# The first modulation vectors computed in two halves of the features, and the token streams loaded ahead of the other transfers

## The chip, the cores and the metric

The kernel runs on one core of a Trainium2 chip. The metric is the device time of one execution in microseconds; a kernel's time is the median of its runs. TensorE (PE in the profile) multiplies matrices, with its weight loads listed apart as PEld; VectorE (DVE) and ScalarE (ACT) work on tiles; GpSimd (POOL) and SyncE (SP) are used here mostly to issue transfers. PEq, ACTq and SPq are the sequencers that issue for these engines. Each engine runs its instructions in the order in which the program was laid out.

## The reference, cut to what matters

The model has two layers and two token streams of 1024 features each: 512 latent tokens (x) and 256 context tokens (ctx). Each layer derives six modulation vectors of 1024 features for each stream from a conditioning vector, and the first thing that a layer does is to normalise each token, scale and shift it by two of these vectors, and multiply the result by one wide input matrix:

```
ml = (silu(c) @ w_ada[l] + b_ada[l]).reshape(B, 6, 1, 1024)      # latent stream
mc = (silu(c_ctx) @ w_ada[l] + b_ada[l]).reshape(1, 6, 1, 1024)  # context stream
hl = rmsnorm(xl, norm1[l]) * (1 + ml[:, 1]) + ml[:, 0]
hc = rmsnorm(xc, norm1[l]) * (1 + mc[:, 1]) + mc[:, 0]
pl, pc = split_in(hl @ w_in[l]), split_in(hc @ w_in[l])
```

Mixing of three kinds, an output product, a gated residual and a feed-forward part follow. w_ada[l] is 1024 x 6144 float32. Vectors 0 and 1 (shift and scale) are wanted at the head of the layer, 2 to 5 much later.

## The kernel before

Tokens lie along the free dimension, features over 128 partitions, so a stream is eight feature tiles (k = 0 to 7) of 128 x 512 (latent) or 128 x 256 (context). Every float32 operand of a large product is cut into a rounded part and a rest (hi and lo), and a product takes three matmuls, hi by hi, lo by hi and hi by lo.

**The modulation vectors** come from `ada(l, g, ring)` (L580). Group g holds two vectors: group 0 is shift and scale of the first norm. Its part of w_ada is 8 MB and comes as 16 tiles of 512 KB: for each half f of the 2048 columns, and each k, one transfer on the queue of SyncE (L588) and matmuls on narrow column strips of TensorE (L590) that sum over k into one bank of PSUM, bank 2 ("a"). In the layout before, half f = 0 is the whole shift vector and f = 1 the whole scale vector. After all 16 tiles one copy brings the bank to SBUF (L594), four transposes turn it (L597), four small additions add the bias (L605), and two operations form gain times (1 + scale) (L611).

**The head of layer 0** is `project` (L691). It loads both streams on the queue of ScalarE (`x_load`, L497: four transfers for each), computes the norm of each stream (`rstd`, L618: squares on ScalarE, sums on VectorE, then `token_rstd` L633 with two steps on TensorE, L637 and L645, which leaves the factors of all tokens in a PSUM bank), runs `ada(0, 0)` to its end with a ring of eight buffers, and then `modulated` (L648) for the context and after it the latent stream: for each k two operations on VectorE (L655, L659) with one on ScalarE between them (L658).

**The token-wise product** is `product_n` (L560), called by `project_dn`: a product with 400 columns in which the tokens of a cell of 128 are the rows. There are six cells, two of context and four of latent tokens, each with an open sum in a bank of its own (0, 1, 3, 4, 5, 6). The weights come in four pieces (k0 = 0, 2, 4, 6), each of two feature tiles; for each piece all six cells get six matmuls (L572, L573, L574), so 144 in all. A piece is loaded (L538), rounded by ScalarE (L540) and its rest formed by VectorE (L541); there are two buffers for each of these steps. When k0 = 6 is done a cell is copied out (`evac`, L727 to L731), with one transfer by GpSimd from one of two small buffers (`ev`). After it come feature-wise products (`product_t`, L544) with convolutions. Beside all this run the 16 tiles of `ada(0, 1)`, with a ring of two buffers.

**Order.** Python generators fix the order of the program; each yields a cost, and `run` (L274) goes on with the one that is furthest behind. On top of that the framework lays out each engine's instructions by a timeline that it simulates: among what is ready it takes the smallest priority number, which grows along the program. `high_priority(n)` and `ahead` (L523) lower the number by n; weight pieces have 500. The order within an engine is fixed then, and on the chip an engine waits at an instruction whose inputs are late, even where later ones are ready. Buffers are found by `Mem` (L173), which prefers those that were freed longest ago.

## Time and profile of the kernel before

| what | us |
|---|---|
| median of 3 runs | 2103.03 (2101.80 to 2104.22) |
| profiled execution | 2102.51 |
| its span, first to last instruction | 2100.70 |
| TensorE busy in the span | 1975.3 (94%) |
| VectorE, ScalarE, GpSimd busy | 1220.2, 858.2, 148.8 |
| mean granted TensorE clock | 0.964 of full speed |

The page gives busy time by engine, then by 40 slices of the span, then DMA, then the chain of work that ended last and the costliest groups of instructions. Ends of matmuls are modelled, so neighbouring matmuls overlap in the listing; the distance between two starts is the better measure of what one takes. Stages are best read from the view by windows, which gives busy time, granted clock and DMA traffic of any stretch, and from the timeline.

### The profile page before, as it was taken

The page shows a single profiled execution, that of the slowest core. Times are in us where ns is not written, and L with a number is a line of the kernel's source. Part 1 is how long each engine was busy: PE and PEld are TensorE (multiplying, and loading weights), DVE is VectorE, ACT ScalarE, POOL GpSimd, SP SyncE. Part 2 cuts the span into 40 slices and gives each one's busy share as a digit, 9 for nine tenths or more (in the row PEclk, how much of TensorE's full clock was granted, in tenths as well). Part 3 has the DMA queues.
Part 4 walks back from the last instruction along what each step waited for, and adds up shares of the span by engine and source line. Part 5 has one row for each costly group of instructions (what it writes and reads, how often), then busy time and mean ns, then how long its engine had stood idle before and what let it go on. Part 6 is the DMA issues. An engine that isn't in the chain of part 4 may idle for free.

```text
span 2100.7 us, 38043 instructions
## 1 busy us (share of the span) xinstructions
PE 1975.3 (94%) x15506; PEld 1626.0 (77%) x15506; DVE 1220.2 (58%) x2761; ACT 858.2 (41%) x1705; POOL 148.8 (7%) x289
## 2 busy tenths in 40 slices
PE   5899999999899999799999998999889979999996
PEld 2787889879899997688788876767678747888885
DVE  4574883756976676766333334756787473333335
ACT  2432354335556563452524232425554234233241
POOL 0001333000000000011000000011200000000000
PEclk9999997999999999899999998999999989999998
DMA  8435343164333242343222245363300222222222
GB/s 338 157 111 166 91 129 105 45 231 152 101 103 110 100 159 86 112 134 118 81 100 90 100 152 173 120 211 131 111 2 12 72 70 91 100 91 100 93 88 81
DMA packets 72831, 242.46 MB, mean 115 GB/s; under 512 B 10320, under 2 KB 13520, under 8 KB 72528
## 3 DMA queue, kind: packets, MB, share of 16 engines
q1 hardware_dynamic: 57456, 196.31, 27.8%
q0 software_dynamic: 12176, 35.19, 5.3%
q10 hardware_dynamic: 3024, 8.53, 1.2%
q8 instruction: 122, 2.00, 0.4%
q14 instruction: 53, 0.43, 0.1%
HBM read 218.21 MB, written 19.14 MB: 113 GB/s over the span
## 4 chain that ended last, share of the span: by engine, by line
PE 79%; DVE 8%; DMA 6%; issue 5%; ACT 2%; POOL 1%; POOLq 0%; ACTq 0%; DVEq 0%; SPq 0%
PE psum L554 20%; PE psum L556 19%; PE psum L555 19%; PE psum L590 2%; PE psum L1457 2%; PE psum L1448 1%; DMA arena<-in_ada 1%; PE psum L1395 1%; PE psum L1122 1%; DVE weights L541 1%; DMA arena<-in_wout 1%; PE psum L1084 1%; DVE arena L1278 1%; DMA r<-in_ada 1%; PE psum L1080 1%
## 5 line engine op out<-in xcount | busy, mean ns | idle before, releaser
L554 PE MATMUL psum<-r,weights 128*128 128x512 f32 (+1 forms) x2288 | 823.2, 361 | 10.8 <-ACT arena L730 3.4
L556 PE MATMUL psum<-r,weights 128*128 128x512 f32 (+1 forms) x2288 | 819.4, 359 | 2.7 <-DVE weights L541 2.5
L555 PE MATMUL psum<-r,weights 128*128 128x512 f32 (+1 forms) x2288 | 817.9, 358 | 0.4 <-DVE r L659 0.3
L540 ACT CAST weights<-arena 128x1024 fp32r<-128x1024 f32 (+3 forms) x295 | 293.7, 996 | 689.1 <-PE psum L555 592.0
L541 DVE TENSOR_TENSOR weights<-arena,weights 128x1024 fp32r<-128x1024 f32 (+3 forms) x295 | 340.8, 1156 | 297.5 <-ACT weights L540 288.8
L554 PEld LDWEIGHTS psum<-r,weights 128*128 128x128 f32 x2288 | 432.3, 189 | 94.7 <-issue 11.1
L556 PEld LDWEIGHTS psum<-r,weights 128*128 128x128 f32 x2288 | 432.1, 189 | 74.1 <-DVE weights L541 6.8
L555 PEld LDWEIGHTS psum<-r,weights 128*128 128x128 f32 x2288 | 432.2, 189 | 68.0 <-issue 3.0
L1514 DVE SCALAR_TENSOR_TENSOR arena<-psum,arena 128x512 f32<-128x512 f32 (+1 forms) x94 | 61.9, 659 | 190.8 <-PE psum L556 190.6
L1501 DVE TENSOR_TENSOR r<-arena,r 128x512 fp32r<-128x512 f32 (+1 forms) x96 | 57.4, 601 | 38.0 <-ACT r L1500 37.7
L658 ACT ACTIVATE r<-arena 128x512 fp32r<-128x512 f32 (+1 forms) x56 | 33.1, 628 | 73.4 <-DVE arena L655 73.4
L590 PE MATMUL psum<-arena 128*32 128x256 f32 x576 | 51.9, 410 | 10.5 <-DMA arena<-in_ada 9.8
L1499 ACT ACTIVATE arena<-arena 128x512 f32<-128x512 f32 (+1 forms) x96 | 54.0, 564 | 2.4
L1500 ACT CAST r<-arena 128x512 fp32r<-128x512 f32 (+1 forms) x96 | 52.8, 553 | 2.4
L1395 PE MATMUL psum<-r 128*128 128x256 f32 (+1 forms) x256 | 52.0, 318 | 0.6 <-ACT r L1428 0.6
L1498 ACT ACTIVATE arena<-psum 128x512 f32<-128x512 f32 (+1 forms) x96 | 50.2, 523 | 0.0
L1485 DVE SCALAR_TENSOR_TENSOR arena<-psum,arena 128x512 f32<-128x512 f32 (+1 forms) x40 | 27.7, 696 | 35.2 <-PE psum L556 34.9
L572 PE MATMUL psum<-weights,r 128*128 128x400 f32 x96 | 34.8, 376 | 10.7 <-DVE arena L655 10.1
L590 PE MATMUL psum<-r,arena 128*32 128x256 f32 x192 | 23.7, 511 | 19.1 <-DMA r<-in_ada 18.9
L655 DVE SCALAR_TENSOR_TENSOR arena<-arena,psum 128x512 f32<-128x512 f32 (+1 forms) x56 | 33.0, 628 | 13.8 <-PE psum L645 13.7
L1453 ACT COPY arena<-psum 128x512 f32<-128x512 f32 x53 | 31.1, 589 | 22.4 <-PE psum L1448 21.9
L1457 PE MATMUL psum<-arena 128*64 128x128 f32 x456 | 37.7, 288 | 2.2 <-ACT arena L1441 2.2
(436 smaller groups left out, 2634.5 us busy)
## 6 DMA issues: line engine op xcount, KB each, us to landing
arena<-in_ff SPq DMA_DIRECT2D x192, 512.0 KB, 3.2
arena<-in_ada SPq DMA_DIRECT2D x72, 512.0 KB, 4.8
arena<-in_win SPq DMA_DIRECT2D x51, 512.0 KB, 3.9
r<-in_ada SPq DMA_DIRECT2D x24, 512.0 KB, 5.5
arena<-in_wout SPq DMA_DIRECT2D x16, 512.0 KB, 3.6
arena<-in_win SPq DMA_DIRECT2D x12, 400.0 KB, 3.6
arena<-in_x ACTq DMA_DIRECT2D x8, 512.0 KB, 7.0
arena<-arena POOLq DMA_DIRECT2D x40, 64.0 KB, 4.5
```

Of the source, the lines that this page charges most:

```text
L540: nc.scalar.copy(hi, st)
L541: nc.vector.tensor_tensor(out=lo, in0=st, in1=hi.bitcast(F32), op=ALU.subtract)
L554: nc.tensor.matmul(o, lhsT=hi[:, w], rhs=h.hi(k), start=k == 0, stop=False)
L555: nc.tensor.matmul(o, lhsT=hi[:, w], rhs=h.lo(k), start=False, stop=False)
L556: nc.tensor.matmul(o, lhsT=lo[:, w], rhs=h.hi(k), start=False, stop=k == nk - 1)
L590: nc.tensor.matmul(ps[32 * j:32 * j + 32, f * 256:f * 256 + 256], lhsT=self.csil[:, k, :], rhs=st[:, j * 256:j * 256 + 256], start=k == 0, ...
L1395: nc.tensor.matmul(o, lhsT=qs[:, kv], rhs=ks[:, kv, a, c0:c1], start=a == 0, stop=a == 1 and not more)
L1457: nc.tensor.matmul(py[heads[kv]], lhsT=self.vS[:, blocks[k0 + kt], heads[kv]], rhs=PT[:, c:c + 128], start=k0 + kt == 0, stop=k0 + kt == n ...
L1499: nc.scalar.activation(out=t, in_=t, func=AF.Square)
L1500: nc.scalar.copy(f.hi(k), t)
L1501: nc.vector.tensor_tensor(out=f.lo(k), in0=t, in1=f.hi(k).bitcast(F32), op=ALU.subtract)
L1514: nc.vector.scalar_tensor_tensor(out=seg.x[m], in0=ps, scalar=self.mod(l, 5, m, seg), in1=seg.x[m], op0=ALU.mult, op1=ALU.add)
```

## The change

The columns of w_ada are laid out anew, for every layer and group: half f of a group's tiles now holds the half f (512 features) of both vectors of the group, instead of the whole of one vector. `ada` is cut into `ada_sums` (the tiles and matmuls of one half) and `ada_out` (two transposes, four bias additions of four columns each, and the products with the gain for that half). Groups other than the first still copy the bank once, and then call `ada_out` twice.

Layer 0 begins with a new function, `project_first`, in place of `project`. The streams are loaded on SyncE's queue with a priority of 2000 instead of on ScalarE's; the tokens' factors are copied from PSUM to SBUF by ScalarE; the first half's eight tiles are summed, its vectors formed (transposes into bank 7, "y"), and the feature tiles k = 0 to 3 of both streams modulated. Then the second half's tiles are summed, with the pieces k0 = 0 and k0 = 2 of the token-wise product set into the program after the second and the sixth of them. After that the second half's vectors and k = 4 to 7 follow, and the rest of the token-wise product is handed to `project_dn`, which runs beside `ada(0, 1)` as before. The streams' buffers are freed only when all tiles are modulated.

```diff
--- before.py
+++ after.py
@@ -155,7 +155,7 @@
     for k, s in PARAM_SHAPES.items():
         assert prm[k].shape == (128,) + s, (k, prm[k].shape)
     o["prm"] = np.concatenate([prm[k].reshape(128, -1) for k in PARAM_SHAPES], axis=1)
-    o["ada"] = w_ada.reshape(DEPTH, 8, 128, 3, 2048).transpose(0, 3, 1, 2, 4)
+    o["ada"] = w_ada.reshape(DEPTH, 8, 128, 3, 2, 2, 512).transpose(0, 3, 1, 2, 5, 4, 6).reshape(DEPTH, 3, 8, 128, 2048)
     o["win"] = np.stack([np.concatenate([_piece(w_in[l][:, IN_COLS[n]]).reshape(-1) for n in IN_NAMES]) for l in range(DEPTH)])
     o["wout"] = np.stack([np.stack([_piece(w_out[l][Y_ROWS][:, 128 * m:128 * m + 128]) for m in range(8)]) for l in range(DEPTH)])
     o["ff1"] = np.stack([np.stack([_piece(w_ff1[l][:, 128 * m:128 * m + 128]) for m in range(32)]) for l in range(DEPTH)])
@@ -489,12 +489,12 @@
         self.wl = Ring(self.wmem, 2, 1024)
 
 
-    def x_load(self, seg):
+    def x_load(self, seg, queue=None):
         seg.xb = [self.get(2 * seg.T, True) for _ in range(4)]
         seg.x = []
         for i, b in enumerate(seg.xb):
             t = b.v.rearrange("p (a t) -> p a t", a=2)
-            self.nc.scalar.dma_start(out=t, in_=seg.home[:, 2 * i:2 * i + 2, :])
+            (queue or self.nc.scalar).dma_start(out=t, in_=seg.home[:, 2 * i:2 * i + 2, :])
             seg.x += [t[:, 0], t[:, 1]]
 
     def x_store(self, seg):
@@ -581,35 +581,44 @@
 
         nc = self.nc
         ps = self.bank("a")
-
         for f in range(2):
-            for k in range(8):
-                st = ring()
-                nc.sync.dma_start(out=st, in_=self.io["ada"][l, g, k, :, f * 1024:f * 1024 + 1024])
-                for j in range(4):
-                    nc.tensor.matmul(ps[32 * j:32 * j + 32, f * 256:f * 256 + 256], lhsT=self.csil[:, k, :], rhs=st[:, j * 256:j * 256 + 256],
-                                     start=k == 0, stop=k == 7, tile_position=(0, 32 * j))
-                yield 2.0
+            yield from self.ada_sums(l, g, f, ring, ps)
         sb = self.get(512)
         nc.vector.tensor_copy(sb.v, ps)
         pt = self.bank("a")
-        for q in range(4):
-            nc.tensor.transpose(pt[:, q * 128:q * 128 + 128], sb.v[:, q * 128:q * 128 + 128], self.ident)
+        for f in range(2):
+            self.ada_out(l, g, f, sb.v, pt[:, f * 256:f * 256 + 256])
         sb.free()
-        m = self.mods[l][:, g * 16:g * 16 + 16, :]
-        src = pt.rearrange("p (f q j r) -> p f j q r", f=2, q=2, j=4)[:, :, :, :, 0:2]
-        b = self.p["b_ada"][:, l, g * 16:g * 16 + 16]
-        for s in range(2):
-            for f in range(2):
-                c = slice(8 * f, 8 * f + 8)
-                nc.vector.tensor_tensor(out=m[:, c, s].rearrange("p (j q) -> p j q", j=4), in0=src[:, f, :, :, s],
-                                        in1=b[:, c].rearrange("p (j q) -> p j q", j=4), op=ALU.add)
+
+    def ada_sums(self, l, g, f, ring, ps):
+
+        nc = self.nc
+        for k in range(8):
+            st = ring()
+            nc.sync.dma_start(out=st, in_=self.io["ada"][l, g, k, :, f * 1024:f * 1024 + 1024])
+            for j in range(4):
+                nc.tensor.matmul(ps[32 * j:32 * j + 32, f * 256:f * 256 + 256], lhsT=self.csil[:, k, :], rhs=st[:, j * 256:j * 256 + 256],
+                                 start=k == 0, stop=k == 7, tile_position=(0, 32 * j))
+            yield 2.0
+
+    def ada_out(self, l, g, f, sb, pt):
+        nc = self.nc
+        for q in range(2):
+            nc.tensor.transpose(pt[:, q * 128:q * 128 + 128], sb[:, f * 256 + q * 128:f * 256 + q * 128 + 128], self.ident)
+        src = pt.rearrange("p (q j r) -> p j q r", q=2, j=4)[:, :, :, 0:2]
+        for v in range(2):
+            c = slice(g * 16 + 8 * v + 4 * f, g * 16 + 8 * v + 4 * f + 4)
+            b = self.p["b_ada"][:, l, c].rearrange("p (j q) -> p j q", j=2)
+            for s in range(2):
+                nc.vector.tensor_tensor(out=self.mods[l][:, c, s].rearrange("p (j q) -> p j q", j=2), in0=src[:, 2 * v:2 * v + 2, :, s], in1=b,
+                                        op=ALU.add)
 
         for w, sc, gain in ((0, 1, "n1"), (1, 4, "n2")):
             if sc // 2 == g:
+                t = slice(4 * f, 4 * f + 4)
                 for s in range(2):
-                    nc.vector.scalar_tensor_tensor(out=self.gmul[l][:, w, :, s], in0=self.mods[l][:, sc * 8:sc * 8 + 8, s], scalar=1.0,
-                                                   in1=self.p[gain][:, l, :], op0=ALU.add, op1=ALU.mult)
+                    nc.vector.scalar_tensor_tensor(out=self.gmul[l][:, w, t, s], in0=self.mods[l][:, sc * 8 + 4 * f:sc * 8 + 4 * f + 4, s],
+                                                   scalar=1.0, in1=self.p[gain][:, l, t], op0=ALU.add, op1=ALU.mult)
 
     def mod(self, l, i, k, seg):
         return self.mods[l][:, i * 8 + k, seg.idx:seg.idx + 1]
@@ -650,14 +659,18 @@
         if pb is None:
             pb = self.rstd(seg)
         h = self.split(seg)
-        for k in range(8):
+        self.modulate(l, which, seg, h, pb, range(8))
+        return h
+
+    def modulate(self, l, which, seg, h, pb, ks):
+        nc = self.nc
+        for k in ks:
             t = self.ev(seg.T)
             nc.vector.scalar_tensor_tensor(out=t, in0=seg.x[k], scalar=self.gmul[l][:, which, k, seg.idx:seg.idx + 1], in1=pb,
                                            op0=ALU.mult, op1=ALU.mult)
             sh = self.mod(l, 3 * which, k, seg)
             nc.scalar.activation(out=h.hi(k), in_=t, func=AF.Identity, bias=sh)
             nc.vector.scalar_tensor_tensor(out=h.lo(k), in0=t, scalar=sh, in1=h.hi(k).bitcast(F32), op0=ALU.add, op1=ALU.subtract)
-        return h
 
 
     def in_piece(self, l, name):
@@ -694,16 +707,54 @@
             if seg.x is None:
                 self.x_load(seg)
         pbs = [self.rstd(seg, "n") for seg in segs]
-        if l == 0:
-            ring = Ring(self, 8, 1024)
-            run(self.ada(0, 0, ring))
-            ring.free()
         for seg, pb in zip(segs, pbs):
             seg.h = self.modulated(l, 0, seg, pb)
+            self.projected(l, seg)
+
+    def projected(self, l, seg):
+        self.x_free(seg)
+        seg.r, seg.b, seg.need = {}, {}, seg is self.lat or l < DEPTH - 1
+        if seg is self.ctx:
+            seg.kv0 = l * 256
+
+    def project_first(self, segs):
+
+        nc = self.nc
+        ab = [self.get(seg.nb * 16, True) for seg in segs]
+        for seg in segs:
+            with self.tc.high_priority(2000):
+                self.x_load(seg, nc.sync)
+        factors = []
+        for seg in segs:
+            pb = self.rstd(seg, "n")
+            factors.append(self.get(seg.T, True))
+            nc.scalar.copy(factors[-1].v, pb)
+        ring = Ring(self, 8, 1024)
+        ps, sb = self.bank("a"), self.get(512)
+        run(self.ada_sums(0, 0, 0, ring, ps))
+        sums = self.ada_sums(0, 0, 1, ring, ps)
+        tokens = None
+        for f in range(2):
+            nc.vector.tensor_copy(sb.v[:, f * 256:f * 256 + 256], ps[:, f * 256:f * 256 + 256])
+            self.ada_out(0, 0, f, sb.v, self.bank("y")[:, 0:256])
+            for seg, b in zip(segs, factors):
+                if f == 0:
+                    seg.h = self.split(seg)
+                self.modulate(0, 0, seg, seg.h, b.v, range(4 * f, 4 * f + 4))
+            if f == 0:
+                for seg, b2 in zip(segs, ab):
+                    seg.r, seg.b, seg.need = {}, {"ab": b2}, True
+                self.ctx.kv0 = 0
+                tokens = self.project_tokens(0, segs)
+                for i, _ in enumerate(sums):
+                    if i in (1, 5):
+                        next(tokens)
+        for seg, b in zip(segs, factors):
             self.x_free(seg)
-            seg.r, seg.b, seg.need = {}, {}, seg is self.lat or l < DEPTH - 1
-            if seg is self.ctx:
-                seg.kv0 = l * 256
+            b.free()
+        sb.free()
+        ring.free()
+        return tokens
 
     def reserve(self, segs, *names):
         for seg in segs:
@@ -717,10 +768,11 @@
     def hs(self, segs, needed=False):
         return [(s, s.h) for s in segs if s.need or not needed]
 
-    def project_dn(self, l, segs):
+    def project_tokens(self, l, segs):
         nc = self.nc
         for seg in segs:
-            seg.b["ab"] = self.get(seg.nb * 16, not seg.need)
+            if "ab" not in seg.b:
+                seg.b["ab"] = self.get(seg.nb * 16, not seg.need)
             seg.r["ab"] = seg.b["ab"].v.rearrange("p (b c) -> p b c", b=seg.nb)
 
         def evac(seg, b, ps):
@@ -731,6 +783,9 @@
             nc.gpsimd.dma_start(out=seg.spill[l][3][b * 128:b * 128 + 128, :], in_=t)
 
         yield from self.product_n(l, "abvi", self.hs(segs), evac)
+
+    def project_dn(self, l, segs, tokens=None):
+        yield from tokens or self.project_tokens(l, segs)
         pad, acc = Ring(self, 2, 512 + 4), Ring(self, 2, 512)
         for i, n in ((1, "k"), (2, "v"), (0, "q")):
             for p in range(2):
@@ -1573,9 +1628,9 @@
                 yield from self.delta_prep(l, seg, seg.need)
 
 
-        self.project(0, both)
+        tokens = self.project_first(both)
         self.reserve((lat, ctx), "dk", "dv", "dq")
-        run(self.project_dn(0, both), (ada(0, 1), 0.7))
+        run(self.project_dn(0, both, tokens), (ada(0, 1), 0.7))
         Ub = self.delta_open(both)
         self.reserve((lat, ctx), "sq0", "sq1")
         run(self.ahead(prep(0, both), 3000), (self.project_swa(0, both), 0.6), (ada(0, 2), 0.7))
```

## Rows read from the trace of the kernel before

**Rows 1.** Windows (start:end, us; busy of each engine, instructions; clock; DMA share, GB/s)

```profile
0.00:2.50 2.50, 0.00 (x0) 0.00 (x0) 0.54 (x2) 0.35 (x1) 1.10 (x9) 1.00 0.33 42
2.50:12.50 10.00, 1.08 (x8) 0.23 (x8) 3.07 (x20) 2.63 (x6) 0.00 (x0) 1.00 0.97 359
12.50:40.00 27.50, 16.02 (x92) 6.32 (x96) 14.31 (x50) 8.37 (x17) 0.00 (x0) 0.85 1.03 410
40.00:81.00 41.00, 35.93 (x264) 29.41 (x260) 23.51 (x54) 16.44 (x32) 1.65 (x3) 0.98 0.53 179
```

**Rows 2.** Timeline of TensorE (start, us taken, line, shape, count, [idle before <-releaser])

```profile
31.77 1.87 PE L637 MATMUL psum<-arena 128*128 128x1 f32 x8 [3.89 <-DVE arena L628]
...
41.62 1.99 PE L590 MATMUL psum<-arena 128*32 128x256 f32 x32
...
46.89 0.45 PE L572 MATMUL psum<-weights,r 128*128 128x400 f32 x1 [0.25 <-ACT r L658]
...
74.13 0.34 PE L573 MATMUL psum<-weights,r 128*128 128x400 f32 x1
...
80.33 0.34 PE L574 MATMUL psum<-weights,r 128*128 128x400 f32 x1
```

**Rows 3.** Timeline of all engines, VectorE's work between the sums and the products

```profile
45.13 0.39 DVE L605 TENSOR_TENSOR arena<-psum,arena 128x8 f32<-128x8 f32 x4 [0.75 <-PE psum L597]
45.44 0.29 DVE L611 SCALAR_TENSOR_TENSOR arena<-arena 128x8 f32<-128x8 f32 x2
45.76 0.87 DVE L655 SCALAR_TENSOR_TENSOR arena<-arena,psum 128x256 f32<-128x256 f32 x2
...
53.24 1.40 DVE L655 SCALAR_TENSOR_TENSOR arena<-arena,psum 128x512 f32<-128x512 f32 x2
...
56.10 1.40 DVE L655 SCALAR_TENSOR_TENSOR arena<-arena,psum 128x512 f32<-128x512 f32 x2
```

**Rows 4.** Groups by line on TensorE, 44 to 81 us (busy us, mean ns | idle before)

```profile
L572 PE MATMUL psum<-weights,r 128*128 128x400 f32 x48 | 16.4, 352 | 0.2 <-ACT r L658 0.2
...
L590 PE MATMUL psum<-arena 128*32 128x256 f32 x64 | 4.9, 390 | 4.0 <-DMA arena<-in_ada 3.5 <-DVE arena L605 0.5
```

**Rows 5.** DMA issues of 0 to 44 us (engine, count, KB each, us to landing)

```profile
arena<-in_ada SPq DMA_DIRECT2D x11, 512.0 KB, 9.3
...
arena<-in_x ACTq DMA_DIRECT2D x4, 512.0 KB, 9.4
arena<-in_win SPq DMA_DIRECT2D x4, 400.0 KB, 7.3
arena<-in_ctx ACTq DMA_DIRECT2D x4, 256.0 KB, 9.2
arena<-in_cst POOLq DMA_DIRECT2D x1, 801.0 KB, 9.8
...
arena<-in_prm ACTq DMA_DIRECT2D x1, 136.0 KB, 4.3
```

**Rows 6.** Chain that ended last, in order of time, one tile at full clock

```profile
110.63 0.57 PE psum L590 x8
```

**Rows 7.** Instructions of line 1441 and who waited for it

```profile
  PE psum L1457: 2.2, 2
```

**Rows 8.** Windows of 2.5 us around two idle stretches of TensorE

```profile
27.50:30.00 2.50, 0.38 (x4) 0.00 (x0) 1.89 (x3) 1.82 (x3) 0.00 (x0) 1.00 1.03 411
...
32.50:35.00 2.50, 2.50 (x22) 1.64 (x21) 1.12 (x7) 0.00 (x0) 0.00 (x0) 0.50 1.02 403
...
40.00:42.50 2.50, 2.50 (x36) 1.26 (x32) 0.00 (x0) 0.00 (x0) 0.00 (x0) 0.64 0.25 92
...
85.00:87.50 2.50, 0.21 (x1) 0.00 (x0) 0.00 (x0) 0.00 (x0) 0.00 (x0) 1.00 1.00 397
...
90.00:92.50 2.50, 2.50 (x7) 1.93 (x7) 0.54 (x4) 1.95 (x4) 0.53 (x1) 0.50 0.00 0
```

**Rows 9.** Timeline of TensorE, the wait behind the copies out of the products

```profile
88.26 0.41 PE L918 MATMUL psum<-r,arena 128*64 128x16 f32 x8 [3.04 <-ACT arena L730]
```

## The prediction

> **What bounds the kernel now.** I read the windows first, then the timelines of the head. TensorE is busy 94% of the span, so little is to be had except where it stands still, and the head is the largest such place: of the first 81 us it is busy 53.0 and idle 28.0 [rows 1], of some 125 us idle in all (span less busy time, from the table). The reader should see three stretches. Up to 40 us the transfers are the bound: 359 GB/s from 2.5 to 12.5 us, then 410 without a break [rows 1], while TensorE only takes tiles of w_ada as they come. The sums end at 43.61 (41.62 + 1.99) [rows 2]. Transposes and small operations take 3.28 us until the first token-wise matmul at 46.89 [rows 2]. Then VectorE is the bound: eight context tiles take it 7.48 us (45.76 to 53.24, or 0.94 a tile), two latent tiles 2.86 (53.24 to 56.10, or 1.43 a tile) [rows 3]. The last of the 144 matmuls starts at 80.33 and is out of the way at 80.5 [rows 2, 4]. So the token-wise products need 33.6 us after the first of them could start, although alone they take 26.3: 34 starts lie between 74.13 and 80.33, so 0.182 us each [rows 2], times 144 [rows 4].
>
> **What the change moves, part by part.** The sum goes by the time at which the last token-wise matmul is out, 80.5 now, with the same work done by then.
>
> *When the first half is there.* What has to move ahead of it: parameters 136 KB, constants 801, context 4 x 256, latent 4 x 512, weight pieces 2 x 400, eight tiles 8 x 512 [rows 5], together 8905 KB or 9.12 MB; with the other two pieces, which also have the smaller priority number, 9.94 MB. By 12.5 us 3.70 MB have moved (42 x 2.5 + 359 x 10, GB/s times us being thousands of bytes) and the rest goes at 410 GB/s [rows 1]: 25.7 or 27.7 us. I take 27.7, since the rounding of the first two pieces is early, and 0.6 us for the last tile's matmuls (0.57 at full clock [rows 6]): 28.3. The bounds are 26.3 and 31, the latter if two tiles of `ada(0, 1)` slip in (1.05 MB). That the streams come through one queue instead of two I cost at nothing: after 12.5 us nearly all the traffic is one queue's, at 410 GB/s. The Trainium skill (DMA: Bandwidth & Descriptors, Specifications) gives a lower limit for reads from HBM, about 358 GB/s for a core; by it the first half would come 2.2 us later. The trace disagrees with it, at 410.
>
> *The norm's factors.* They now come early: the streams are whole after 4.11 MB, about 13.5 us. The two TensorE steps and the small chain between them began at 31.77 now and were over before the last tiles' matmuls at 41.62 [rows 2], so under 9.9 us; with 1.5 us for the last squares and sums they end by 25, some 3 us ahead of the first half. What goes away is TensorE's wait of 3.89 us for the latent sums, behind which tiles of w_ada had piled up [rows 2]. The two copies of factors on ScalarE have that slack as cover; without it they cost about 1 us.
>
> *First product.* 3.28 us after the sums now; the copy and the transposes are half as long, so 3.0: 31.3 us. The bias and gain operations keep their number per half (four of 0.10 us, two of 0.15 [rows 3]). For each of the five later groups one more set of four, and for three of them two more with the gain, run: 5 x 0.4 + 3 x 0.3 = 2.9 us of VectorE, which is busy 58% of the span; nothing by that cover, 2.9 without it.
>
> *A wait that is added.* The first half's copy reads bank 2 while the second half's matmuls sum into other columns of it. The trace has the like: L1441 reads columns 128 to 255 of a bank, L1457 writes 0 to 127, and waits for it [rows 7]. So the second half's first tile waits behind the copy, with every matmul queued behind it: 0.5 to 0.9 us. Tiles land every 1.28 us (512 KB at 410 GB/s) and take 0.57, so this is made up by the second tile: 0.
>
> *From 31.3 on.* TensorE has left: 26.3 us of products; the second half's tiles less the two that landed before, 6 x 0.57 = 3.4 [rows 6]; and the tiles of `ada(0, 1)` that lay before 80.5, seven of the eight after 44 us (64 matmuls at eight a tile) [rows 4], 4.0. That is 33.7, hence 65.0 if it never stands still. VectorE does not bound it: four context and four latent tiles are 9.5 us (4 x 0.94 + 4 x 1.43), so the first half is done at about 39.7, ahead of products that take 13.1 us and the tiles between; the second half's data are there at 38 (14.1 MB) and its tiles would be done by 53. What is open is whether the last second-half tiles come ahead of the k0 = 2 products in TensorE's order or after them. Ahead: no gap, 65.0. After: the sums end when the first half's products do, 3.0 us pass before the next product, 68.0. I take the middle, and half a microsecond for the start of the latent tiles: 67.0. **Gain: 80.5 - 67.0 = 13.5 us**, 12 to 15.5 with these ends. Weight pieces three and four need buffers that the k0 = 0 and k0 = 2 products free some 10 us before they are wanted, against about 2 us to round them: nothing.
>
> *Behind 81 us.* What is late next is the copying out of six cells through two buffers, which makes TensorE wait 3.04 us now [rows 9]; it hangs on the last piece's products and moves along with them. From there TensorE is the bound nearly everywhere, so I carry the whole gain to the end. The layout of everything later is made anew by the simulated timeline; I give it 3 us either way, the size of that one wait.
>
> The profiled execution is 2102.51 (span 2100.70 and 1.81 around it), 0.5 under the median. 2102.5 - 13.5 = 2089.0.
>
> **The rivals.**
>
> *The clock drops in the new overlap.* After TensorE had stood for 3.89 us its granted clock was 0.50 of full speed, the lower level, from 32.5 to about 41 us; after a wait of 3.04 us it was 0.50 again at 90 to 92.5 [rows 2, 8, 9]. The new kernel has a pause of about 3 us before its first product, unless second-half tiles fill it. A dip of 10 us costs 5: 2094. Against it: tiles keep landing every 1.28 us, and with single tiles from 12.5 us on the clock held: its mean of 0.85 over 12.5 to 40 [rows 1] is 8.3 us at 0.50, and the dip after 30 us accounts for that. The Trainium skill (TensorE: Matmul & The Clock Gate, HAM oscillation — how this bites in real kernels) says that idle gaps between bursts bring the lower clock back; by that rule this pause would too, and 2094 would be the likelier time. The trace bears it out for gaps of 3 and 3.9 us without any matmul.
>
> *Slower.* The same dip, lasting, with the second half's tiles behind the products. If the clock stays at 0.50 from 31.3 until the second half's sums end, 13.1 us of products and 3.4 of tiles take 33.0; sums end at 64.3, the next product is at 67.3, and 13.1 + 4.0 follow: 84.4, so 3.9 us later than now, 2106.4. It decides from about 27 us of half clock, which take the 13.5 away. The trace shows none longer than about 10 us in the head.
>
> *The overlap does not come.* If the fixed order puts the first half's tiles and products behind the second half's tiles, the change gives only the earlier end of the sums: all bytes have moved at 38 (14.14 MB), so 39.0 instead of 43.61: 4.6 us, 2098. For it: TensorE does wait in a fixed order for late inputs, 3.89 us for the latent sums with tiles of w_ada landed behind them [rows 2]. Against: VectorE has nothing else to do then, and if only the products are held, they start at 39 with modulated tiles waiting: 39.0 + 26.3 + 4.0 = 69.3, still 11 us.
>
> *Given back.* The gain appears at 81 us and a new wait of the later layout takes 10 or more: within 2099 to 2106. Nothing in the trace prices it beyond the 3 us above.
>
> **How the numbers follow.** Forecast 2089 (2086 to 2092, with the layout 2083 to 2095): 0.57. Dip, 2094: 0.17. No overlap, 2098: 0.09. Given back, about 2101: 0.10. Slower, 2106: 0.07. About 0.2%, 4.2 us, is what a measurement of this kernel can tell from no change. Faster: 0.57 + 0.17 + most of 0.09 = 0.82; same: the rest of that and given back, 0.11; slower 0.07. The range reaches from 2083 to the no-overlap case, 2099, and leaves out the last two.
>
> **What would show it.** Right: first token-wise matmul near 31 us and the last near 67; modulated tiles (L655's operation) beside traffic at 410 GB/s; idle time of TensorE before 81 us down by about 13 us and much the same after it. Wrong: a first product near 39 or later (order); a granted clock of 0.50 between 30 and 50 us (dip); streams landing after 16 us (the one queue is slower); TensorE idle between 45 and 50 us (second vectors late); idle time after 81 us up by several microseconds (given back).

## The result and the profile after

| | before | after |
|---|---|---|
| median, us | 2103.49 (4 runs, 2101.80 to 2104.22) | 2090.87 (4 runs, 2089.18 to 2093.16) |
| ratio after to before | | 0.9946 (95%: 0.9934 to 0.9959) |
| profiled execution, us | 2102.51 | 2089.67 |
| its span | 2100.70 | 2087.80 |
| TensorE busy in the span | 1975.3 | 1975.2 |
| TensorE idle (span less busy) | 125.4 | 112.6 |
| mean granted clock | 0.964 | 0.964 |

The change makes the kernel about 12.6 us faster, against 2089.0 foretold. TensorE's busy time is the same to 0.1 us; the whole difference is idle time. So the first question is where the idle time went. New line numbers: the ada tiles are L600, their transposes L607, squares L636, sums L637, the two steps of the norm on TensorE L646 and L654, the copy of the factors L731, the copy of the vectors L738, modulation L669 to L673, copying out L780 and L782; the product lines keep theirs.

The windows of after, cut as [rows 1] (start and end; length, then busy time and instructions of PE, PEld, DVE, ACT, POOL; clock, DMA share, GB/s):

```profile
0.00:2.50 2.50, 0.00 (x0) 0.00 (x0) 0.54 (x2) 1.28 (x1) 1.10 (x9) 1.00 0.19 40
2.50:12.50 10.00, 0.00 (x0) 0.00 (x0) 3.57 (x25) 2.38 (x8) 0.00 (x0) 1.00 0.99 357
12.50:40.00 27.50, 16.65 (x118) 6.88 (x118) 16.58 (x57) 9.23 (x17) 0.55 (x1) 0.88 1.03 410
40.00:81.00 41.00, 39.37 (x265) 31.85 (x258) 23.07 (x53) 20.37 (x41) 2.87 (x6) 1.00 0.51 177
```

From 40 to 81 us TensorE now stands for 1.63 us instead of 5.07, but from 12.5 to 40 it still stands for 10.85 (11.48 before), where the first products were to fill it. Before 81 us the idle time fell by 3.0 us, from 27.97 to 24.98, and not by 13. The timeline of TensorE in after (start, time taken, line, shapes, count, idle before and its releaser) shows why:

```profile
28.56 1.05 PE L646 MATMUL psum<-arena 128*128 128x1 f32 x8 [1.21 <-DVE arena L637]
29.54 0.64 PE L600 MATMUL psum<-arena 128*32 128x256 f32 x8
33.27 2.05 PE L654 MATMUL psum<-arena 128*128 128x512 f32 x2 [3.09 <-DVE arena L652]
35.24 1.08 PE L600 MATMUL psum<-r,arena 128*32 128x256 f32 x8
36.26 0.69 PE L607 MATMUL psum<-arena 128*128 128x128 f32 x2
...
38.80 0.45 PE L572 MATMUL psum<-weights,r 128*128 128x400 f32 x1 [0.50 <-ACT r L672]
...
55.13 1.06 PE L600 MATMUL psum<-arena 128*32 128x256 f32 x12
56.71 0.44 PE L607 MATMUL psum<-arena 128*128 128x128 f32 x2 [0.53 <-DVE arena L738]
...
59.15 0.45 PE L572 MATMUL psum<-weights,r 128*128 128x400 f32 x1 [1.00 <-ACT r L672]
...
74.62 0.34 PE L574 MATMUL psum<-weights,r 128*128 128x400 f32 x1
```

The first half's sums end at 30.2 (29.54 + 0.64), but its transposes (L607) run at 36.26 and the first product starts at 38.80 (46.89 before [rows 2]). Between them stands the latent stream's second norm step, L654 at 33.27, for which TensorE waits 3.09 us and behind which the tiles and the transposes are queued. The last token-wise matmul starts at 74.62 (80.33 before), 5.7 us earlier; five tiles of `ada(0, 1)` lie before it instead of seven, so at equal work it is 4.6 us (5.7 less 2 x 0.57 [rows 6]).

So the head gave a third of the 13 us by the measure of the prediction. To find the rest I cut the span where TensorE reaches the same matmul in both kernels: the 160th, 1700th and 1900th matmul of L554, the first of the three products of every feature-wise product. The windows of after, cut there (columns as above):

```profile
0.00:203.60 203.60, 178.35 (x1200) 131.77 (x1200) 121.69 (x340) 67.05 (x130) 13.61 (x49) 0.95 0.57 199
203.60:1453.10 1249.50, 1206.75 (x9815) 1015.12 (x9812) 763.99 (x1727) 544.77 (x1083) 111.44 (x204) 0.97 0.37 122
1453.10:1788.60 335.50, 307.25 (x3226) 248.18 (x3225) 227.01 (x573) 149.99 (x364) 19.59 (x28) 0.94 0.20 66
1788.60:2087.80 299.20, 282.81 (x1273) 232.11 (x1271) 113.21 (x155) 98.78 (x131) 4.33 (x8) 0.97 0.27 92
```

The same cuts in the kernel before:

```profile
0.00:212.40 212.40, 179.10 (x1208) 134.05 (x1208) 119.42 (x328) 66.86 (x129) 13.51 (x49) 0.94 0.55 191
212.40:1458.30 1245.90, 1206.29 (x9795) 1012.59 (x9792) 760.30 (x1707) 541.71 (x1081) 111.78 (x205) 0.97 0.37 122
1458.30:1801.40 343.10, 307.05 (x3237) 247.21 (x3236) 227.31 (x572) 150.92 (x365) 19.15 (x28) 0.94 0.20 64
1801.40:2100.70 299.30, 282.84 (x1273) 232.15 (x1271) 113.18 (x155) 98.71 (x131) 4.34 (x8) 0.98 0.27 92
```

Length less the first number after it is TensorE's idle time in each part:

| part, by matmuls of L554 | idle before | idle after | difference |
|---|---|---|---|
| up to the 160th | 33.3 | 25.3 | -8.1 |
| 160th to 1700th | 39.6 | 42.8 | +3.1 |
| 1700th to 1900th (layer 1's mixing) | 36.1 | 28.3 | -7.8 |
| 1900th to the end | 16.5 | 16.4 | -0.1 |
| all | 125.4 | 112.6 | -12.8 |

The first part holds the 3.0 us before 81 us and 5.1 behind it: 5.33 us of idle time from 81 us on (33.30 less 27.97) became 0.27 (25.25 less 24.98). The 3.04 us wait of [rows 9] is most of that: the matmul that waited there for a copying-out (L918, now L973) starts in after without a wait.

```profile
79.67 0.41 PE L973 MATMUL psum<-arena 128*64 128x16 f32 x8
```

The other large difference, 7.8 us, lies some 1400 us behind the head. The rewritten lines of `ada` run for later groups too, the last of them at 1426 us (L620 of after); the part from 1453 us on has the same work in both kernels.

### The profile page after: what moved, and what is told of

Its sections match the earlier page's. It is cut to its first block, busy times and chain, and to the rows that moved or that the text cites. A ratio compares the mean times of both kernels' runs of the same rounds, so it can differ in the third digit from the quotient of the medians.

```text
span 2087.8 us, 38082 instructions
## 1 busy us (share of the span) xinstructions
PE 1975.2 (95%) x15506; PEld 1627.2 (78%) x15506; DVE 1225.9 (59%) x2794; ACT 860.6 (41%) x1707; POOL 149.0 (7%) x289
## 4 chain that ended last, share of the span: by engine, by line
PE 66%; issue 22%; DVE 5%; DMA 4%; ACT 2%; POOL 0%; SPq 0%; POOLq 0%; ACTq 0%; DVEq 0%
PE psum L554 15%; PE psum L556 15%; PE psum L555 14%; PE psum L600 3%; PE psum L1512 2%; PE psum L1503 2%; PE psum L1450 2%; DMA arena<-in_ada 1%; DMA r<-in_ada 1%; PE psum L1177 1%; PE psum L1329 1%; PE psum L1135 1%; PE psum L572 1%; PE psum L574 1%; PE psum L1139 1%
## 5 line engine op out<-in xcount | busy, mean ns | idle before, releaser
L554 PE MATMUL psum<-r,weights 128*128 128x512 f32 (+1 forms) x2288 | 823.9, 361 | 10.7 <-ACT arena L782 3.3
L554 PEld LDWEIGHTS psum<-r,weights 128*128 128x128 f32 x2288 | 432.9, 189 | 96.1 <-issue 13.3
L1556 DVE TENSOR_TENSOR r<-arena,r 128x512 fp32r<-128x512 f32 (+1 forms) x96 | 57.5, 601 | 36.1 <-ACT r L1555 35.8
L572 PE MATMUL psum<-weights,r 128*128 128x400 f32 x96 | 35.9, 386 | 11.9 <-DVE arena L669 10.1
L600 PE MATMUL psum<-arena 128*32 128x256 f32 x448 | 40.0, 406 | 3.3 <-DMA arena<-in_ada 3.1
L1503 PE MATMUL psum<-arena,r 128*128 128x128 f32 x180 | 36.4, 291 | 7.0 <-ACT r L1480 6.3
L1508 ACT COPY arena<-psum 128x512 f32<-128x512 f32 x53 | 31.2, 590 | 25.8 <-PE psum L1503 25.4
L600 PE MATMUL psum<-r,arena 128*32 128x256 f32 x320 | 33.6, 461 | 7.5 <-DMA r<-in_ada 7.5
L1450 PEld LDWEIGHTS psum<-r 128*128 128x128 f32 x256 | 38.4, 198 | 2.7 <-issue 0.9
```

The costliest lines, as they stand in the source:

```text
L554: nc.tensor.matmul(o, lhsT=hi[:, w], rhs=h.hi(k), start=k == 0, stop=False)
L572: nc.tensor.matmul(ps[:, :w], lhsT=h.hi(k)[:, t], rhs=hi[:, c], start=k == 0, stop=False)
L600: nc.tensor.matmul(ps[32 * j:32 * j + 32, f * 256:f * 256 + 256], lhsT=self.csil[:, k, :], rhs=st[:, j * 256:j * 256 + 256], start=k == 0, ...
L1450: nc.tensor.matmul(o, lhsT=qs[:, kv], rhs=ks[:, kv, a, c0:c1], start=a == 0, stop=a == 1 and not more)
L1503: nc.tensor.transpose(pt[:, c:c + 128], Ps[kv][:, (k0 + kt) * 128:(k0 + kt) * 128 + 128], self.ident)
L1556: nc.vector.tensor_tensor(out=f.lo(k), in0=t, in1=f.hi(k).bitcast(F32), op=ALU.subtract)
```

## The experiments

Two questions were open. **First**, why the norm's factors came late. Theory A: two small buffers. `rstd` puts each square after the first into one of the two `ev` buffers, and `token_rstd` puts the diagonal matrix of the factors into one as well, so the second such square of the latent stream waits until TensorE has used the context's matrix. Theory B: the copies of the factors, which the change adds, stand ahead of the latent squares in ScalarE's order. ScalarE's timeline in after fits both: its latent squares stop at 17.93 and go on at 23.23, right behind the context's step on TensorE and its copy.

```profile
17.30 0.63 ACT L636 ACTIVATE arena<-arena 128x512 f32<-128x512 f32 x1
...
22.96 0.37 ACT L731 COPY arena<-psum 128x256 f32<-128x256 f32 x1 [4.29 <-PE psum L654]
23.23 0.63 ACT L636 ACTIVATE arena<-arena 128x512 f32<-128x512 f32 x1
...
35.35 0.59 ACT L731 COPY arena<-psum 128x512 f32<-128x512 f32 x1 [7.78 <-PE psum L654]
```

**Second**, whether the gain is the overlap in the head, or comes from a part of the change or from the new layout of what follows. All times below are medians with the ratio to the kernel before and its 95% interval; all profiled idle times are span less TensorE's busy time.

**Copies behind both norms (copies_late).** From the changed kernel:

```diff
-        factors = []
+        factors, pbs = [], []
...
-            pb = self.rstd(seg, "n")
+            pbs.append(self.rstd(seg, "n"))
...
-            nc.scalar.copy(factors[-1].v, pb)
+        for b, pb in zip(factors, pbs):
+            nc.scalar.copy(b.v, pb)
```

> Edit: the two copies of the tokens' factors on ScalarE stand behind the norms of both streams in the program instead of each behind its own. In the changed kernel the first half's sums end at 30.2 us but the first token-wise matmul starts at 38.8, because the latent factors are copied only at 35.9. Three theories for that. A (buffers): the latent squares use two small buffers, one of which holds the context stream's diagonal matrix until TensorE's second step for it at 22.9, and so stand still; this edit then changes the first matmul by less than 1 us. B (order): ScalarE's copy of the context factors stands ahead of the latent squares and holds them 4.3 us; this edit brings the first matmul to about 34. C (transfers): the first half's data are the bound and the factors are not; no change. Total: within 5 us of the changed kernel in any case, since the layout of everything later is made anew.

Measured: 2088.78 us, 0.9932 (0.9910 to 0.9954); first product 38.63, last 74.62. The head did not move, so theory B falls.

**Matrices in a place of their own (dg_own).** The diagonal matrices go to a stretch of an array (`kT`) that nothing else holds then:

```diff
-        dg = self.ev(T)
+        dg = self.ev(T) if dg is None else dg
...
-            pb = self.rstd(seg, "n")
+            pb = self.rstd(seg, "n", self.kT[:, 512 * seg.idx:512 * seg.idx + seg.T])
```

> Edit: the diagonal matrices of the two norms at the head get memory of their own (the keys' buffer, idle then) instead of one of the two small buffers that the squares use. A (buffers): the latent squares run on from 17.9 instead of standing until 23.2, the latent factors are ready about 5 us earlier, at 31, and the first token-wise matmul starts at 33 to 35 instead of 38.8. B (order): ScalarE still waits at the copy of the context factors; no change. C (transfers): no change, since the first half's sums end at 30.2 either way and 8.6 us follow. The last token-wise matmul moves by 3 to 5 us under A (74.6 now), and the total by as much, give or take the later layout.

Measured: 2089.40 us, 0.9939 (0.9917 to 0.9960); first product 33.61, last 76.46. ScalarE's timeline of this kernel: the latent squares run on without TensorE, the last at 21.52.

```profile
17.14 1.14 ACT L636 ACTIVATE arena<-arena 128x512 f32<-128x512 f32 x2
...
21.52 0.63 ACT L636 ACTIVATE arena<-arena 128x512 f32<-128x512 f32 x1 [0.94 <-DVE arena L637]
27.21 0.37 ACT L731 COPY arena<-psum 128x256 f32<-128x256 f32 x1 [5.05 <-PE psum L654]
30.17 0.58 ACT L731 COPY arena<-psum 128x512 f32<-128x512 f32 x1 [2.59 <-PE psum L654]
```

And TensorE's:

```profile
31.34 0.41 PE L607 MATMUL psum<-arena 128*128 128x128 f32 x2 [0.64 <-DVE arena L738]
33.61 0.45 PE L572 MATMUL psum<-weights,r 128*128 128x400 f32 x1 [1.85 <-ACT r L672]
...
52.35 1.07 PE L600 MATMUL psum<-arena 128*32 128x256 f32 x16
...
54.73 0.44 PE L607 MATMUL psum<-arena 128*128 128x128 f32 x2 [1.31 <-DVE arena L738]
```

Theory A holds: the first product is 5.2 us earlier. The end of the head is not, it is 1.8 us later, and the time is not apart from after's: the second half's last tiles run at 52.35, behind all 72 products of the first half, and the second half's vectors are then the bound.

**The second half's tiles ahead of the k0 = 2 products in the program (sums_ahead).**

```diff
-                    if i in (1, 5):
+                    if i in (1, 7):
```

> Edit: in the program the second piece of the token-wise product stands behind all of the second half's tiles, not behind six of them. In the changed kernel the last tile's matmuls run at 55.1, behind all products of the first half, though the transfers went quiet at 45; then 4.3 us pass between the last product of the first half and the first of the second, with two tiles of the next group in them. Order theory: the last tile's matmuls run before 50, the pause at 55 is gone, and the last token-wise matmul ends 2 to 4 us earlier than 74.8; total about 3 us lower. Rival (TensorE has no more to do there anyway, tiles of the next group only fill in elsewhere): the last product moves by under 1 us.

Measured: 2107.72 us, 1.0021 (1.0004 to 1.0037); first product 38.44, last 77.04. The last tile came at 50.41 but the transposes only at 55.85, with products between them, so only half of the intended order came about and the head is 2.4 us later than after's. The time is 16.9 us above after's, though, and most of that is not the head: its profiled execution has 8.4 us more idle time than after's (121.0) and TensorE busy 9.3 us longer (1984.5) with the same 15506 matmuls. From the 1700th to the 1900th matmul of L554 alone it is idle 33.5 us, 5.3 more than after. One digit in the program's order costs more behind the head than in it.

**No products inside the loop of sums (products_held).**

```diff
-                for i, _ in enumerate(sums):
-                    if i in (1, 5):
-                        next(tokens)
+                for _ in sums:
+                    pass
```

> Edit: no product is put beside the second half's tiles; the first half's feature tiles are still modulated beside them. It tells what the overlap of VectorE's work alone is worth. Prediction's theory (products need only be ready to run without a gap, VectorE was the bound): the first product starts when the second half's sums are in, about 46, and the last ends at 75 to 77, so 0 to 2 us later than in the changed kernel. Rival (the early products carry the gain): the last ends about where it did before the change, at 80.

Measured: 2087.33 us, 0.9934 (0.9910 to 0.9958); first product 38.94, last 74.42. The products came as early as before the edit: the framework's layout takes what is ready, wherever it stands in the program. So this says nothing on what the overlap is worth.

**Both waits of the head mended (dg_own_prio2).** The matrices as in dg_own, the second half's sums with a raised priority, its copy and vectors with a higher one:

```diff
-                for i, _ in enumerate(sums):
-                    if i in (1, 5):
-                        next(tokens)
+                for i in (0, 1):
+                    next(tokens)
+                with self.tc.high_priority(400):
+                    for _ in sums:
+                        pass
...
+            with self.tc.high_priority(600 * f):
```

> Edit: diagonal matrices in memory of their own as in dg_own, and in the program both early pieces of the token-wise product, then the second half's tiles with a priority of 400 and its copy, transposes and small operations with 600. In dg_own the first product came at 33.7 but the last at 76.5, because the second half's last two tiles stand behind all 72 early products in TensorE's order (52.4 us, though transfers went quiet at 45) and the vectors after them. Order theory: here the last tile's matmuls run before 50, the second half's first product by 54, and the last token-wise matmul ends at 71 to 73.5. Rival (VectorE or the weight pieces bound the second half): last product still at 75 or later. Total 2 to 5 us under dg_own, give or take the later layout (6 us).

Measured: 2090.59 us, 0.9932 (0.9916 to 0.9948); first product 34.67, the second half's first at 56.16 (59.15 in after), last 73.71. That is 0.9 us ahead of after's last product, and the time is not apart from after's.

**The column layout and the cut of `ada` alone (halves_alone).** The kernel before, with half f holding half of both vectors and `ada_sums` and `ada_out`, but `project` as it was:

```diff
-    o["ada"] = w_ada.reshape(DEPTH, 8, 128, 3, 2048).transpose(0, 3, 1, 2, 4)
+    o["ada"] = w_ada.reshape(DEPTH, 8, 128, 3, 2, 2, 512).transpose(0, 3, 1, 2, 5, 4, 6).reshape(DEPTH, 3, 8, 128, 2048)
```

> Edit: the kernel before with only the new layout of w_ada's columns and the small operations cut in two (eight bias additions for four, in every group); nothing is overlapped and the streams load as before. It is the control for the claim that a part of the change's gain is chance of the later layout and not the head's. Chance theory: the head stays (first token-wise matmul 46.9, last 80.3, each within 1 us), yet the time from there to the end differs from the kernel before by several microseconds either way, as in the four kernels run before this one, in which the stretch between the 1500th and the 1900th matmul of line 554 took 558 to 572 us (567 before, 561 with the change) with no edit near it. Rival (the gain behind the head is caused by the change itself): total within 2 us of the kernel before, plus at most 2.9 for the added operations.

Measured: 2113.65 us, 1.0047 (1.0029 to 1.0064); last product 81.79. Nothing in the head explains 10 us: it is 1.5 us later there. Idle in the part from the 1700th to the 1900th matmul of L554: 39.6 us, 3.5 more than before; up to the 160th it is 4.2 us less, from there to the 1700th 5.7 more. In all its profiled execution has 5.1 us more idle time (130.5), and TensorE is busy 5.1 us longer (1980.4).

**The early streams alone (streams_alone).** The kernel before, with the streams on SyncE's queue and a priority of 2000:

```diff
-            self.nc.scalar.dma_start(out=t, in_=seg.home[:, 2 * i:2 * i + 2, :])
+            (queue or self.nc.scalar).dma_start(out=t, in_=seg.home[:, 2 * i:2 * i + 2, :])
...
-            if seg.x is None:
+            if seg.x is None and l == 0:
+                with self.tc.high_priority(2000):
+                    self.x_load(seg, self.nc.sync)
+            elif seg.x is None:
```

> Edit: the kernel before with only the streams' loads moved to SyncE's queue ahead of all else; the first modulation vectors come whole. If the early streams are worth something by themselves, it is the end of the sums: 43.6 us before, 39 to 42 here, since TensorE no longer stands at the latent sums with tiles landed behind it; the last token-wise matmul then ends 2 to 4 us ahead of 80.5. If the two small buffers decide here too, the latent step on TensorE is at 33 to 36 and nearly nothing is won: last product within 1 us of 80.5. Total: as much, give or take the later layout (6 us).

Measured: 2107.05 us, 1.0013 (1.0003 to 1.0023); first product 48.69, last 85.61, so 1.8 and 5.3 us later than in the kernel before, against both expectations. The profiled execution is the slowest of its ten (2111.93), so part of that may be its own. Alone, this part gains nothing.

**The streams late, everything else as in the change (streams_late).**

```diff
-            with self.tc.high_priority(2000):
-                self.x_load(seg, nc.sync)
+            self.x_load(seg)
```

> Edit: the change with the streams loaded as before, on ScalarE's queue with no priority; the halves and their overlap stay. If early streams are what brings the first half's tiles forward, the latent factors come at 39 to 41 as before the change and the first token-wise matmul at 42 to 44 instead of 38.8, the last about 3 us later than 74.8. If the small buffers set the latent norm's time whatever the loads do, both stay within 1.5 us.

Measured: 2096.65 us, 0.9960 (0.9946 to 0.9974); first product 44.29, last 80.67, hardly earlier than before the change (46.89 and 80.33). The early streams are worth 6.0 us of head in the combination, because without them the factors come later still (L654 for the latent stream at 37.90 instead of 33.27). And with no gain left at the last product the kernel is still 0.4% faster than before, with 27.9 us idle in the far part. Some of the gain is not of the head.

**The buffers alone (before_mem).** The kernel before in its order, but with buffers taken and freed as the change does: the token-wise product's result buffers first, a spare buffer in place of each factor copy, the copy of the vectors held, the streams and the ring freed late.

```diff
+        if l == 0:
+            return self.project_0(segs)
...
+    def project_0(self, segs):
+        ab = [self.get(seg.nb * 16, True) for seg in segs]
...
+            spare.append(self.get(seg.T, True))
+        ring = Ring(self, 8, 1024)
+        sb = self.get(512)
+        run(self.ada(0, 0, ring, sb))
...
+        for seg, b in zip(segs, spare):
+            self.x_free(seg)
+            b.free()
```

> Edit: the kernel before with its head unchanged in work and order, but with buffers taken and given back as the change does: the small 'ab' buffers first, a spare buffer for each stream's factors, one buffer for the sums' copy, and both streams' buffers freed only when all tiles are modulated. In the stretch between the 1700th and the 1900th matmul of line 554 (layer 1, attention beside the delta chain) TensorE stood still 36.0 us before, 28.3 with the change; it was 27.9 to 30.1 in five other kernels with the new head, 33.5 in sums_ahead, 36.0 and 39.6 in the two with the old head. Memory theory: the placement of buffers decides which instructions wait for one another there; this kernel then has 30 or less in that stretch and is 5 to 8 us faster than the kernel before, with the head as before (first token-wise matmul at 46.9). Order theory: it is the laying out by the simulated timeline, which answers to any edit; the stretch then takes some other value, anywhere from 28 to 40 us. Rival (caused by the earlier head): 36 us as before.

Measured: 2099.47 us, 0.9968 (0.9949 to 0.9987); first product 47.73, last 79.50. The windows, cut at the same matmuls:

```profile
0.00:211.10 211.10, 178.46 (x1208) 133.53 (x1208) 119.51 (x328) 67.05 (x129) 13.58 (x50) 0.97 0.57 192
211.10:1456.90 1245.80, 1205.82 (x9795) 1012.20 (x9792) 762.53 (x1707) 544.29 (x1081) 112.07 (x205) 0.97 0.38 122
1456.90:1799.20 342.30, 312.27 (x3237) 249.01 (x3236) 227.77 (x572) 150.94 (x365) 19.23 (x28) 0.94 0.20 65
```

Up to the 160th matmul it is idle 32.6 us, as before the change (33.3); from the 1700th to the 1900th 30.0, near after's 28.3 and 6.0 less than before. So that part does not need the overlap. In all it is idle 6.3 us less (119.1), but TensorE was busy 4.2 us longer in this execution (1979.5), so its span is only 2.1 us shorter. That it is the placement of the buffers which brings the 6.0 us, and not the new layout that any edit may bring, this one control does not show: 30.0 also lies in the 28 to 40 of the order theory. For the buffers speaks that all nine profiled executions that have them lie at 27.9 to 33.5 us, and the four without them at 36.0 to 39.6; eight of the nine have the new head as well.

**The two kernels again, unedited (after_again, before_again).**

> The changed kernel once more, unedited, to tell what of the 7.7 us less idle time of TensorE between the 1700th and the 1900th matmul of line 554 is this execution's chance. If the fixed order makes it, the idle time is 28.3 again within 1.5 us, and so the head: first token-wise matmul 38.8, last 74.6. If it is chance of one execution, it differs by several microseconds.

> The kernel before once more, unedited, for the same question: 36.0 us of idle time of TensorE between the 1700th and the 1900th matmul of line 554 within 1.5 us if the fixed order makes it, and a first token-wise matmul at 46.9, a last at 80.3.

Measured: after_again 2087.40 us, 0.9936 (0.9916 to 0.9956); before_again, one execution, 2099.9. The idle time repeats: 36.4 us in the far part for before_again (36.1) and 28.8 for after_again (28.3); 125.9 and 113.5 in all (125.4 and 112.6). So the far difference is in the order of the program and not in the chance of an execution. The head repeats less well: after_again has its first product at 39.06 but its last at 76.34, not at 74.6, with a granted clock of 0.50 from 60 to 62.5 us; before_again has 47.10 and 80.02. By this pair the last product is 3.7 us earlier, not 5.7.

What TensorE waits for in the far part, in the kernel before (line, tile, releaser: us in total, times, longest):

```profile
PE psum L1448 <- ACT arena L1453: 5.2, 5, 3.0
PE psum L1202 <- DVE r L1194: 4.0, 1, 4.0
...
PE psum L1448 <- ACT r L1425: 2.8, 2, 1.5
```

In after, where L1448 is L1503 and L1453 is L1508:

```profile
PE psum L1503 <- ACT r L1480: 6.3, 3, 4.1
...
PE psum L1503 <- ACT arena L1508: 0.7, 1, 0.7
```

In before_mem, where they are L1470 and L1475:

```profile
PE psum L1470 <- ACT r L1447: 3.3, 3, 1.5
...
PE psum L1470 <- ACT arena L1475: 1.1, 2, 0.7
...
PE psum L1224 <- DVE r L1216: 0.8, 1, 0.8
```

Two waits of the kernel before, 9.2 us together, are 0.7 us in after and 1.9 in before_mem: transposes of attention's weights that wait for the copy of the transposes before them, and transposes of the delta part's output that wait for VectorE (L1202, now L1257 in after and L1224 in before_mem; there they also wait for another operation of VectorE, 1.7 and 1.6 us). Another wait of the same transposes, for the exponentials (L1425, now L1480), grew by 3.5 us in after. Which buffer's place made the layout choose another order there was not traced and stays open.

## Why the prediction was right, and where it was not

The total came out within 2 us, 12.8 us in the profiled executions against 13.5 by the sum, and the forecast overlap in the head did come about. But by the prediction's own signs the sum was made up of the wrong pieces: the last product is earlier by 5.7 us, 4.6 at equal work, and the rest of the gain lies behind 81 us, where the prediction put nothing. That the total is so close is in good part luck, an error in each direction.

- **When the first half is there: right.** 28.3 foretold, 30.2 found, within the bounds of 26.3 to 31. The transfers ran at 410 GB/s from 12.5 to 40 us, through the one queue. The lower limit that the prediction quoted from the Trainium skill (DMA: Bandwidth & Descriptors, Specifications) is again not what binds here; the same page (Bandwidth, Measured) gives higher figures for a core that streams alone, and this trace, with one core and 410, agrees with that place.
- **The norm's factors: this step failed.** "They now come early ... they end by 25, some 3 us ahead of the first half." The streams did come early, but the latent factors were in place at 35.9 instead of by 25 (L654 of after from 33.27 to 35.32, the copy at 35.35 with 0.59), and the first product came 7.5 us late, at 38.80 instead of 31.3. I took the 9.9 us between two TensorE steps as an upper bound for the latent chain and left out what its squares wait for. The trace of before showed it, on ScalarE: a latent square that follows a TensorE step of the context.

```profile
26.05 0.63 ACT L627 ACTIVATE arena<-arena 128x512 f32<-128x512 f32 x1 [2.67 <-PE psum L645]
```

  dg_own showed the cause, the shared `ev` buffers, and gave 5.2 us of the 7.5 back. The other 2.3 are the end of the sums, 30.7 in that kernel against 28.3 foretold; from there to its first product it takes 2.9 us, against 3.0. The estimate of 25 was wrong by more than that wait, though: in dg_own too the latent factors are in place only at 30.75 (30.17 + 0.58). The prediction gave 1.5 us to the last squares and sums after the streams had landed, so it had them done at 15; in dg_own VectorE ends the latent sums at 23.08, taking 0.69 for each of seven, with the context's steps and the rests of two weight pieces between them. There this holds nothing back, since the first half's sums end at 30.7.

```profile
22.39 0.69 DVE L637 TENSOR_TENSOR arena<-arena 128x512 f32<-128x512 f32 x1
```

- **From the first product to the last: right.** For the case that the last second-half tiles come behind the k0 = 2 products the sum has 36.7 us with seven tiles of `ada(0, 1)`, 35.6 with five; found are 35.8 between the first and the last start, with five. That case is also the one that came: the last tiles at 55.13, behind the 72 products that end at 55. sums_ahead and dg_own_prio2, meant to bring the other case, got half of the order and 0.9 us of the end; a forecast in the middle of the two was 1 us too early.
- **The added wait for the PSUM bank: 0, as foretold, but not tested in after.** TensorE stood behind L654 at that time, so the wait that was priced could not appear. In streams_late it does, with 0.55 us, within the 0.5 to 0.9 of the prediction: the second half's first tile waits for the copy of the first half's sums (L737 there).

```profile
35.64 1.08 PE L600 MATMUL psum<-r,arena 128*32 128x256 f32 x8 [0.55 <-DVE arena L737]
```

- **The later wait: wrong.** "It hangs on the last piece's products and moves along with them." The wait of L918 did not move along, it vanished, 3.04 us, with some 2 us of other idle time before the 160th matmul. On ScalarE the wait of the copying-out for its transfer is 1.9 us in after and 4.8 in before. An earlier end of the products is not what does it: in streams_late the last product ends no earlier than before the change (80.67), yet between 81 us and the 160th matmul TensorE is idle for 0.2 us, as in after (0.3). Nor is it the buffers alone (5.0 in before_mem) or the early streams alone (3.8 in streams_alone); the column layout alone leaves 2.0. All executions of a kernel with the new head have 0.2 to 0.5. What in the new head does it stays open: the traffic around differs, and so does the order of TensorE's work.
- **The layout behind the head: the term that was mis-sized.** I gave it 3 us either way. In the far part alone it was -7.8 in after, -6.0 in before_mem, +3.5 in halves_alone; between the 160th and the 1700th matmul it was +3.1 in after. Whole kernels with the same head work differ by as much as the gain: +10 us for halves_alone, 16.9 between sums_ahead and after. The result lies even within the narrow range of 2086 to 2092, but not because this was seen: the layout brought what the head fell short of.
- **The rivals.** The dip came in part: the granted clock was 0.50 around the wait for L654, while TensorE worked off its tiles. There L654 took 2.05 us and the tile behind it 1.08 (0.57 at full clock [rows 6]); half of these and of the transposes is some 2 us, an estimate, ahead of the first product. It was over when the products began, so 2094 did not come. The prediction's argument against the dip, that the clock held with single tiles, rests on a misread row: the tile at 13.11 of before takes 1.08 us, as long as the one at 33.56 under a clock of 0.50; the 1.00 printed around it is no record (see the last section). The windows of after:

```profile
30.00:32.50 2.50, 0.18 (x4) 0.00 (x0) 2.16 (x14) 0.00 (x0) 0.00 (x0) 0.66 1.03 406
32.50:35.00 2.50, 1.73 (x2) 0.50 (x2) 0.62 (x4) 0.00 (x0) 0.00 (x0) 0.50 1.02 406
35.00:37.50 2.50, 2.50 (x19) 0.89 (x22) 0.45 (x6) 0.59 (x1) 0.55 (x1) 0.50 1.05 415
```

  "The overlap does not come" was near: a fixed order did hold the transposes and tiles behind a late input, and the sign set for it ("a first product near 39 or later") is what the trace shows, but the products of the first half still ran ahead of the second half's vectors. "Given back" did not happen in after; with sums_ahead it did, in full. "Slower" did not.

So, of 12.8 us: 3.0 us of idle time went before 81 us and 5.1 just behind it, the latter with the new head but not through an earlier end of the products; 3.1 came back before the 1700th matmul, and 7.8 went in a part whose work the change leaves as it was. before_mem, with no overlap, has a ratio of 0.9968, so some half of the gain (0.32% of 0.54% to 0.64%, with wide intervals) is to be had with the new buffers and without the overlap. No version that was run is apart from the changed kernel on the fast side: copies_late, products_held and dg_own_prio2 have intervals that overlap that of after_again.

## What to carry to other kernels

Before a step that moves work forward is priced, follow each input of the moved work back through the small buffers that it shares: two buffers for squares and matrices tied one stream's norm to the other's, and were worth 5 us of the first product, though none of the total, since the second half then set the end. Where an order is laid out anew by a planner, a local sum can be right and the total still be set elsewhere: cut both traces at the same matmul numbers, compare idle time part by part, and run a control that has the new buffers and none of the new overlap. Price such a layout by what controls show, here several microseconds in either direction, and not by the size of one wait.

## What the hardware showed that was not expected

The clock after a pause is not the same in every execution of one kernel. TensorE of before waits 3.04 us ahead of the matmul at 88.26 and then has 0.50 of full speed from 90 to 92.5, where 7 matmuls begin [rows 8, 9]. In before_again it waits 2.98 us at the same place and the clock stays at 1.00; 12 matmuls begin in the same window. The durations agree with the clock: a 128x512 matmul at 90 us takes 0.63 us in before and 0.40 in before_again. First the row of before, then the wait and the window of before_again:

```profile
90.53 0.63 PE L556 MATMUL psum<-r,weights 128*128 128x512 f32 x1
```

```profile
87.89 0.41 PE L918 MATMUL psum<-r,arena 128*64 128x16 f32 x8 [2.98 <-ACT arena L730]
```

```profile
90.00:92.50 2.50, 2.50 (x12) 2.03 (x11) 0.78 (x5) 1.57 (x4) 0.56 (x1) 1.00 0.00 0
```

The Trainium skill (TensorE: Matmul & The Clock Gate, HAM oscillation — how this bites in real kernels) lets such a gap bring the lower clock back; one execution agrees and the other does not, so a pause makes a dip possible here and not certain. The price of this one is 1.6 us: from that matmul to the one of L934, with the same 21 products between, it is 6.86 us in before and 5.31 in before_again.

The printed clock has to be held against durations, too. Ahead of 31.77 TensorE of before waits 3.89 us, and the windows then print 0.50 [rows 2, 8]; in before_again it waits 3.90 us there and the windows print 1.00. But the same work takes the same time in both, 1.87 us for L637 and 1.08 for the tile behind it:

```profile
31.79 1.87 PE L637 MATMUL psum<-arena 128*128 128x1 f32 x8 [3.90 <-DVE arena L628]
```

```profile
32.50:35.00 2.50, 2.50 (x22) 1.66 (x22) 1.10 (x7) 0.00 (x0) 0.00 (x0) 1.00 1.00 398
```

The trace's record of the clock begins at 28.1 us in before and at 42.2 in before_again, and the windows print 1.00 where there is no record. Until then both ran as slowly as under 0.50: a tile of before takes 1.08 us at 13.11 and at 33.56, and 0.57 at full clock [rows 6].

```profile
13.11 1.08 PE L590 MATMUL psum<-r,arena 128*32 128x256 f32 x8 [0.62 <-DMA r<-in_ada]
...
33.56 1.08 PE L590 MATMUL psum<-arena 128*32 128x256 f32 x8
```

So the head of the two executions ran alike, with the first product at 46.89 and 47.10, and a mean granted clock that covers the head is too high. Over the span TensorE's busy time for the same kernel differs by 3 us between two executions (1975.3 and 1972.1 for before, 1975.2 and 1972.1 for after), while its idle time repeats within 1 us. For a change of half a per cent the idle time of one profile is therefore the steadier measure than its span.
